# The products with w and u in the chunked delta-rule scan: one product of 128 columns with w, products with u in turn

## The chip, the cores and the metric

The kernel runs on one core of a Trainium2 chip. The metric is device time in microseconds (us), the median of three runs. Its engines in the profile are PE (TensorE matmul; PEld is its weight load), DVE (VectorE), ACT (ScalarE), POOL (GpSimd) and SP (SyncE, which here issues most DMAs). A float32 matmul appears in the trace as two records.

## The reference

A network of two blocks over 1024 tokens. The first block has gated scans, a dilated attention and a second layer of gated scans. The second block has, beside a pooling branch, a state-space scan (SSD) and a delta-rule scan (GDN) of six heads, both in two directions, then a router and experts. The change concerns the delta-rule scan, whose core is this:

```python
def gdn_chunked(q, k, v, g, beta, s0):
    ...
    u = jnp.einsum('bnhij,bnhjv->bnhiv', tm, vc * bc[..., None])
    w = jnp.einsum('bnhij,bnhjk->bnhik', tm, kb * jnp.exp(gc)[..., None])
    attn = jnp.einsum('bnhik,bnhjk->bnhij', qc, kc) * decay
    qg = qc * jnp.exp(gc)[..., None]
    kend = kc * jnp.exp(gc[..., -1:] - gc)[..., None]
    gend = jnp.exp(gc[..., -1])

    def step(s, inp):
        u_i, w_i, a_i, qg_i, ke_i, ge_i = inp
        v_new = u_i - jnp.einsum('bhlk,bhkv->bhlv', w_i, s)
        o_i = jnp.einsum('bhlk,bhkv->bhlv', qg_i, s) + jnp.einsum('bhij,bhjv->bhiv', a_i, v_new)
        s = s * ge_i[..., None, None] + jnp.einsum('bhlk,bhlv->bhkv', ke_i, v_new)
        return s, o_i
```

Chunks hold 64 tokens. The kernel folds w and u into matrices ahead of the walk over chunks: a chunk's end state is (exp(g_end) - ke^T w) S + ke^T u, and its outputs are (q exp(g) - A w) S + A u, with A the masked and decayed products of queries and keys.

## The kernel before, in words

All work is on one core. Matmul operands of the large projections are split into exact high and low parts (L139 to L141, three products for one). The framework schedules the instructions of the whole program into one fixed order per engine before the run, by its own estimate of times and with priority for what frees PSUM (`g.up()`); on the chip each engine runs its list in that order and waits on semaphores. Thus an edit in one function can shift instructions of others.

The stage in question begins near 2857 us of the span. `latent_mixers` calls `gdn_scan` for three pairs of heads (hp 0, 1, 2), `ssd` (the state-space scan), `gdn_finish` and then `MixersOut.group` for the output projection. `gdn_scan` loads keys and values and transposes them (L1556), multiplies queries with keys (L1571, tile hkq) and calls `prepare(d)` for both directions. `prepare` multiplies values and keys with the inverse T (L1603), so that huw holds u and hwb holds w as blocks of 128x128. From there:

- hke, keys decayed to the chunk's end (L1612, GpSimd), and hA, the diagonal of the state's factor (L1615);
- L1620: products of w with hke, 64 columns for each pair of chunks and head; L1623 subtracts them from hA;
- L1628: products of hke with u, halves of 64 partitions to the other half's partitions, copied into hB by L1635;
- the decay row of all chunks into hx (L1639 calls `gdn_rows`, four DMAs): exp and product with the queries (L1641, L1642, tile hQ), subtraction (L1643), mask (L1647, GpSimd), exp (L1649), product with hkq (L1650, GpSimd);
- L1654: products of w with those rows, subtracted from hQ by L1657; L1663: products of the rows with u, copied or added into hO by L1667 and L1669.

`carry` then walks over the chunks (L1692, L1694: one small product and one addition per chunk) and adds the states' part to the outputs (L1708). It runs beside the next pair's `prepare`. The state-space scan runs beside all of this (srow, sxw, sxb, sBC and L1245 to L1353). PSUM has three banks for the large projections (mm), one for the carry (a), and two each of o and tr, which `bank()` hands out in turn. Of `pool.tile` the argument bufs is the number of buffers of a tag: a writer waits until the reader of the buffer's earlier content is done.

Of the kernel before, what the change touches and what calls it, by code (L numbers as in the profile page):

```python
# [27 lines left out]
def dap(ap, dims, off=0):  # L28
    """A DRAM access pattern over ap's tensor, dims in elements."""
    return bass.AP(tensor=ap.tensor, offset=ap.offset + off, ap=[list(d) for d in dims])  # L30


class Ctx:
    """Engines, pools and constants shared by the parts."""
# [32 lines left out]
    def open_w(self):  # L67
        """Room for weight blocks, on the left; closed by ws.close()."""
        self.w = self.ws.enter_context(self.pool("w"))
# [18 lines left out]
    def psum(self, tag):  # L88
        """A bank of the tag's; work set aside to fill gaps has one of its own."""
        tag = self.aside or tag  # L90
        return self.ps.tile([P, 512], F32, name=tag, tag=tag, bufs=self.banks[tag])

    def psum_pool(self, name, **banks):
        """A pool of PSUM with the given numbers of banks, to be entered."""
# [7 lines left out]
    def load_w(self, blk, scale=None, k=4, n=256, units=2, colscale=None, pool=None, bufs=2):  # L102
        """A weight block [128, units*k, n] in DRAM, as exact float32r high and low parts."""
# [23 lines left out]
    def up(self):  # L127
        """For what frees PSUM."""
        return self.tc.high_priority()
# [5 lines left out]
    def mm3(self, ps, sta, mov, first=True, last=True):  # L135
        """ps += sum_k sta[k]^T mov[k], each a (hi, lo) pair of float32r operands."""
# [7 lines left out]
def fm(w, c, X, t0, n=512):  # L144
    """Operands of a feature-major product: 128 features at column c of block w, n tokens from t0."""
# [4 lines left out]
def tm(w, X, t0):  # L150
    """Operands of a token-major product: 128 tokens from t0, all columns of block w."""
# [3 lines left out]
class Gated:  # L155
    """The bidirectional gated scan of one head with its norm and gate, in units of n tokens.

    Backward units come first, from the last; then forward units, each followed by its outputs."""
# [11 lines left out]
    def unit(self, d, u, q, k, lg):  # L170
        """Direction d (0 forward, 1 backward), unit u; q, k, lg: [128 keys, n], lg: log gates / gs.
        Returns the forward outputs' decayed q."""
# [19 lines left out]
        # decays of the chunks, and the factors that carry q and k over neighbouring ones  # L192
# [18 lines left out]
        # states  # L211
# [30 lines left out]
        # products within the groups  # L242
# [21 lines left out]
    def out(self, u, qd, St, G, y):  # L264
        """Outputs of unit u into y [128 tokens, group, Vd]: head rms norm and gate."""
# [48 lines left out]
def put_y(g, pool, ydram, chunk, t0, src, tag="y_hl", bufs=1):  # L314
    """A piece of y^T, 128 features, tokens from t0: split exactly and kept in DRAM."""
# [6 lines left out]
def attention_pair(g, pool, ydram, pair, qs, qps, kT, gate, vd, bias, spread, before):  # L322
    """Two heads (128 features) of the dilated attention, from feature-major q (times -1/8), per head with the
    other's rows zero (qps: room for it by residues, likewise), k and silu(gate); vd: v in DRAM [1024, 512]; bias[h][p]: minus the biases, tiles [128, 256] or [128, 64].
    Returns what is left to do, the sum of the patterns; before: what the pair before left."""
# [8 lines left out]
    def permuted(d):  # L334
        """q and k with their tokens by residue of d"""
# [8 lines left out]
    # values, tokens on partitions in each pattern's order  # L344
# [122 lines left out]
    # weights of the patterns, in tokens' order: rows (h, j), j the block of 128 tokens  # L467
# [40 lines left out]
    def rest():  # L508
        # the weights, one row per 128 tokens, brought to the head's partitions by a product
# [16 lines left out]
def load_xT(g, pool, src):  # L526
    """x^T [1024, 1024] as eight chunks of features, exact high and low parts."""
# [29 lines left out]
def rel_bias(g, pool):  # L557
    """Minus the relative biases per head and pattern: tiles [query, key - query + 64]."""
# [13 lines left out]
    # a copy of each row per query, so that a pitch one shorter reads them shifted  # L572
# [21 lines left out]
def sigmoid(g, dst, src):  # L594
    """1 / (1 + exp(-src)), by the functions that share a table with the scans' own."""
# [16 lines left out]
class Layer0:  # L612
    """Layer 0: the gated scans' heads, and what the attention takes, into DRAM: per pair of heads q, k and gate by
    features; v by tokens; the biases."""

    def __init__(self, g, es, X, ydram):
# [6 lines left out]
        # low-rank gate inputs, split and stacked for one pass: rows hi, hi, lo  # L623
# [23 lines left out]
    def feature(self, dst, w, evict):  # L647
        """128 features into DRAM"""
# [6 lines left out]
    def inputs(self, c):  # L655
        """A pair's part of what the attention takes, and half of the values or of the gates."""
# [16 lines left out]
    def project(self, h):  # L673
        """A head's projections into DRAM"""
# [62 lines left out]
    def heads(self, hs, after, side="left"):  # L737
        """The scans of some heads; after(h) adds what may fill their gaps."""
# [36 lines left out]
class OutProj:  # L775
    """z = alpha x + y W, over groups of chunks of 128 features."""
# [6 lines left out]
    def load(self, chunks, pool=None, parts=1):  # L783
        """[y^T of the chunk, its weights], each high and low parts; pool: for further weights."""
# [39 lines left out]
    def last(self, chunks, more, pool, finish):  # L824
        """Chunks, some more with their weights in pool; finish(tok) when a tile of tokens is done."""
# [8 lines left out]
def layer_norm(g, zp, zt, gain, bias):  # L834
    """zt [128 tokens, 1024] in place."""
# [16 lines left out]
def to_feature_major(g, zt, tok, X, tags=("a", "o")):  # L852
    """Transpose 128 tokens [128, 1024] into the chunks X (exact high and low parts, or whole)."""
# [12 lines left out]
def hgrn(g, hp, X, ydram, aside):  # L866
    """Layer 1: twelve heads of 128 keys and values."""
# [992 lines left out]
class MixersOut:  # L1860
# [44 lines left out]
    def close(self):  # L1905
        self.es.close()
# [539 lines left out]
```

## Time and profile before

| | |
|---|---|
| runs | 3773.04, 3778.67, 3780.81 us; median 3778.67 us |
| profiled execution | span 3765.8 us; no time of its own beside the span is listed |
| PE busy | 3383.4 us, 90% of the span |
| DVE, ACT, POOL busy | 2579.5, 1618.4, 1444.7 us |
| DMA | 461.05 MB, mean 122 GB/s |
| scan stage | about 2860 to 3240 us |

A timeline row is a run of like instructions, with its start, the time from that start to the end of the last, the engine, the line, the tiles (out<-in), the shape and the number of records; in brackets the engine's idle time before it and what ended it. Matmuls are pipelined, so the start of the next row tells more of the pace than the duration. PEclk is the granted clock: 1.0 is 2.4 GHz and 0.5 is 1.2 GHz.

### The profile page before, as it was taken

The page shows a single profiled execution, that of the slowest core. Times are in us where ns is not written, and L with a number is a line of the kernel's source. Part 1 is how long each engine was busy: PE and PEld are TensorE (multiplying, and loading weights), DVE is VectorE, ACT ScalarE, POOL GpSimd, SP SyncE. Part 2 cuts the span into 40 slices and gives each one's busy share as a digit, 9 for nine tenths or more (in the row PEclk, how much of TensorE's full clock was granted, in tenths as well). Part 3 has the DMA queues.
Part 4 walks back from the last instruction along what each step waited for, and adds up shares of the span by engine and source line. Part 5 has one row for each costly group of instructions (what it writes and reads, how often), then busy time and mean ns, then how long its engine had stood idle before and what let it go on. Part 6 is the DMA issues. An engine that isn't in the chain of part 4 may idle for free.

```text
span 3765.8 us, 59868 instructions
## 1 busy us (share of the span) xinstructions
PE 3383.4 (90%) x21896; PEld 2754.0 (73%) x21896; DVE 2579.5 (68%) x5580; ACT 1618.4 (43%) x3340; POOL 1444.7 (38%) x1437
## 2 busy tenths in 40 slices
PE   7998998999988999999999999688896879858897
PEld 6886886777667888888898977566675868636665
DVE  4767664265476685977767686669995565578787
ACT  3443333444624454545545451344443331235565
POOL 4556664000023233434333331623213563245553
PEclk9998999999898999999999999889896889869999
DMA  5222244252333111111111234224337465578994
GB/s 182 75 82 90 88 136 139 79 174 66 89 119 106 64 65 59 50 59 48 50 43 63 68 123 148 81 87 133 105 106 174 111 157 182 214 214 291 299 326 152
DMA packets 374051, 461.05 MB, mean 122 GB/s; under 512 B 150483, under 2 KB 280787, under 8 KB 373756
## 3 DMA queue, kind: packets, MB, share of 16 engines
q1 hardware_dynamic: 359916, 407.93, 34.3%
q0 software_dynamic: 13840, 49.29, 4.4%
q8 instruction: 173, 2.83, 0.3%
q14 instruction: 122, 1.00, 0.1%
HBM read 357.57 MB, written 104.27 MB: 123 GB/s over the span
## 4 chain that ended last, share of the span: by engine, by line
PE 61%; DVE 16%; issue 7%; DMA 6%; POOL 4%; ACT 4%; SPq 2%; DVEq 0%; POOLq 0%; ACTq 0%
PE mm L139 12%; PE mm L140 12%; PE mm L141 12%; DVE cacc L1137 2%; PE a L247 2%; DVE elo L2015 2%; PE o L225 1%; DMA srow<-rdsl 1%; PE o L276 1%; PE a L214 1%; PE a L141 1%; PE a L251 1%; PE a L140 1%; PE o L280 1%; PE o L278 1%
## 5 line engine op out<-in xcount | busy, mean ns | idle before, releaser
L116 POOL TENSOR_TENSOR wlo<-wraw,whi 128x1024 fp32r<-128x1024 f32 (+1 forms) x131 | 329.0, 2516 | 537.1 <-ACT whi L115 532.4
L2013 ACT CAST ehi<-eraw 128x1024 fp32r<-128x1024 f32 x192 | 200.3, 1050 | 148.7 <-PE a L141 95.9
L139 PE MATMUL mm<-x1h,whi 128*128 128x512 f32 x576 | 237.4, 412 | 7.9 <-DVE G L913 3.5
L140 PE MATMUL mm<-x1l,whi 128*128 128x512 f32 x576 | 234.6, 407 | 2.5 <-DVE x1l L133 2.5
L141 PE MATMUL mm<-x1h,wlo 128*128 128x512 f32 x576 | 234.8, 408 | 0.0
L139 PE MATMUL mm<-whi,x1h 128*128 128x256 f32 x768 | 222.2, 289 | 0.0
L141 PE MATMUL mm<-whi,x1l 128*128 128x256 f32 x768 | 219.8, 287 | 0.0
L140 PE MATMUL mm<-wlo,x1h 128*128 128x256 f32 x768 | 219.6, 286 | 0.0
L2015 DVE TENSOR_TENSOR elo<-eraw,ehi 128x1024 fp32r<-128x1024 f32 x138 | 193.3, 1435 | 31.6 <-ACT ehi L2013 31.2
L115 ACT CAST whi<-wraw 128x1024 fp32r<-128x1024 f32 (+1 forms) x131 | 136.1, 1040 | 167.1 <-PE mm L140 96.9
L2017 POOL TENSOR_TENSOR elo<-eraw,ehi 128x1024 fp32r<-128x1024 f32 x54 | 138.2, 2565 | 167.4 <-ACT ehi L2013 153.2
L139 PE MATMUL mm<-whi,xh 128*128 128x256 f32 x640 | 185.2, 290 | 0.0
L140 PE MATMUL mm<-wlo,xh 128*128 128x256 f32 x640 | 183.9, 288 | 0.5 <-POOL wlo L116 0.5
L141 PE MATMUL mm<-whi,xl 128*128 128x256 f32 x640 | 183.2, 286 | 0.0
L139 PE MATMUL mm<-x2h,whi 128*128 128x512 f32 x400 | 165.4, 413 | 13.0 <-ACT cu L1129 8.8
L140 PE MATMUL mm<-x2l,whi 128*128 128x512 f32 x400 | 164.9, 412 | 0.0
L141 PE MATMUL mm<-x2h,wlo 128*128 128x512 f32 x400 | 163.2, 409 | 0.8 <-POOL wlo L116 0.8
L139 PE MATMUL mm<-whi,yin 128*128 128x512 f32 x352 | 149.4, 428 | 14.4 <-DVE z L816 6.9
L816 DVE TENSOR_TENSOR z<-z,mm 128x512 f32<-128x512 f32 x144 | 97.7, 682 | 86.8 <-PE mm L141 86.4
L139 PE MATMUL mm<-xh,whi 128*128 128x512 f32 x336 | 138.0, 411 | 19.3 <-ACT whi L115 16.2
L239 POOL TENSOR_TENSOR u_qh<-u_qa,facX 128x256 f32<-128x256 f32 x64 | 71.3, 1114 | 202.7 <-DVE u_qa L236 172.5
L139 PEld LDWEIGHTS mm<-whi,x1h 128*128 128x128 f32 x768 | 146.9, 191 | 1.1
(756 smaller groups left out, 10832.0 us busy)
## 6 DMA issues: line engine op xcount, KB each, us to landing
eraw<-in_we_gate_dram SPq DMA_DIRECT2D x64, 512.0 KB
eraw<-in_we_up_dram SPq DMA_DIRECT2D x64, 512.0 KB
eraw<-in_we_down_dram SPq DMA_DIRECT2D x64, 512.0 KB
yin<-yd POOLq DMA_DIRECT2D x29, 1024.0 KB, 9.1
aw<-in_ada_w_dram SPq DMA_DIRECT2D x96, 256.0 KB
yd<-y_hl SPq DMA_DIRECT2D x80, 256.0 KB
wraw<-in_w_dram SPq DMA_DIRECT2D x25, 512.0 KB
wraw<-in_w_out_dram SPq DMA_DIRECT2D x24, 512.0 KB
```

Source lines behind the costliest of these rows:

```text
L115: nc.scalar.copy(hi[:, :sz], raw[:, :sz])
L116: nc.gpsimd.tensor_tensor(lo[:, :sz], raw[:, :sz], hi[:, :sz].bitcast(F32), op=ALU.subtract)
L139: nc.tensor.matmul(ps, sh, mh, start=first and i == 0, stop=False)
L140: nc.tensor.matmul(ps, sh, ml, start=False, stop=False)
L141: nc.tensor.matmul(ps, sl, mh, start=False, stop=last and i == n - 1)
L239: nc.gpsimd.tensor_tensor(v3(qh, 32), v3(qa, 32), bcast(fqh, nck, 32), op=ALU.mult)
L247: nc.tensor.matmul(ap[:, o:o + P], w(kt, 0, P), w(qt, 0, P), start=True, stop=True)
L816: nc.vector.tensor_add(zz, zz, ps)
L1137: nc.vector.scalar_tensor_tensor(acc, u[:, i:i + n], cw[:, i:i + 1], acc, op0=ALU.mult, op1=ALU.add)
L2013: nc.scalar.copy(hi, raw)
L2015: nc.vector.tensor_sub(lo, raw, hi.bitcast(F32))
L2017: nc.gpsimd.tensor_tensor(lo, raw, hi.bitcast(F32), op=ALU.subtract)
```

## The change

In `prepare`, keys and rows lie side by side in one tile of the latents' scan (tag hke, 8 KB per partition instead of 4, still one buffer), and one product with w of 128 columns serves both. The row's chain (load, exp, subtraction, mask, exp, product) moves ahead of that product, and its last step writes into the shared tile. The products with u for the state (L1655 after) and for the outputs (L1658 after) alternate chunk by chunk and head by head in two banks. In the context's scan, which needs no outputs, the products stay as they were. Two buffer counts shrink: hf from 2 to 1, and the raw weights of the output projection (mraw) from 3 to 2. Everything else in the diff removes comments.

```diff
-        f = pool.tile([P, 3, ncp, 2], F32, name="hf", tag="hf", bufs=2)
+        f = pool.tile([P, 3, ncp, 2], F32, name="hf", tag="hf", bufs=1)
...
-        ke = t4("hke")
+        kinds = 1 if fin is not None else 2
+        kr = big("hke", [ncp, 2, kinds, 64])
+        ke = kr[:, :, :, 0]
         nc.gpsimd.tensor_tensor(ke, kt, bc(f[:, 0]), op=ALU.mult)
+        if fin is None:
+            row = gdn_rows(g, pool, n, rows, hp, d, 0, "hx", 2)
+            Q = big("hQ", [2, ncp, 64], 4)
+            nc.scalar.activation(Q, row, AF.Exp)
+            nc.vector.tensor_mul(Q, Q, qE)
+            nc.vector.tensor_sub(row, row, hc(col))
...
+            at = kr[:, :, :, 1]
+            nc.gpsimd.tensor_tensor(at.rearrange("p c h i -> p h c i"), row, kq, op=ALU.mult)
         A = t4("hA", two)
...
+        per = 4 // kinds
+        for q0 in range(0, ncp, per):
+            mm = min(per, ncp - q0)
+            ps = bank()
+            wd = kinds * 64
+            for i in range(mm * 2):
+                cp, h = q0 + i // 2, i % 2
+                nc.tensor.matmul(ps[:, i * wd:(i + 1) * wd], wb[:, cp * 2 + h], kr[:, cp, h], start=True, stop=True)
+            p5 = ps[:, :mm * 2 * wd].rearrange("p (c h x i) -> p c h x i", h=2, x=kinds, i=64)
+            with g.up():
+                nc.vector.tensor_sub(A[:, q0:q0 + mm], A[:, q0:q0 + mm], p5[:, :, :, 0])
+                if fin is None:
+                    Qs = Q[:, :, q0:q0 + mm].rearrange("p h c i -> p c h i")
+                    nc.vector.tensor_sub(Qs, Qs, p5[:, :, :, 1])
         for q0, mm in step4:
             ps = bank()
+            po = bank() if fin is None else None
             for i in range(mm * 2):
                 cp, h = q0 + i // 2, i % 2
-                nc.tensor.matmul(ps[:, i * 64:i * 64 + 64], wb[:, cp * 2 + h], ke[:, cp, h], start=True, stop=True)
...
+                io = slice(i * 64, i * 64 + 64)
                 for e in range(2):
+                    nc.tensor.matmul(ps[half[1 - e], io], ke[half[e], cp, h], u(e, cp, h), start=True, stop=True)
+                if fin is None:
+                    for e in range(2):
+                        nc.tensor.matmul(po[half[e], io], at[half[e], cp, h], u(e, cp, h), start=True, stop=True)
...
-        nc.gpsimd.tensor_tensor(row, row, kq, op=ALU.mult)
-        for h in range(2):
-            ps = bank()
-            for cp in range(ncp):
-                nc.tensor.matmul(ps[:, cp * 64:cp * 64 + 64], wb[:, cp * 2 + h], row[:, h, cp], start=True, stop=True)
...
-                raw = zp.tile([P, 512], F32, name="mraw", tag="mraw", bufs=max(nb, 2))
+                raw = zp.tile([P, 512], F32, name="mraw", tag="mraw", bufs=2)
```

PE's order in the first pair of heads, first direction, before (here one row is one instruction, x the number of them):

```order
L1620 MATMUL tr<-hke,hwb 128x64 x8
L1628 MATMUL o<-huw,hke 64x64 x16
L1248 MATMUL mm<-ident,sXB 128x128 x3
L1254 MATMUL mm<-ident,sXB 128x128 x2
L1620 MATMUL tr<-hke,hwb 128x64 x8
L1628 MATMUL o<-huw,hke 64x64 x2
L1692 MATMUL a<-hS,hA 64x64 x2
L1628 MATMUL o<-huw,hke 64x64 x14
L1265 MATMUL mm<-sxw,sxb 128x192 x2
L1654 MATMUL tr<-hx,hwb 128x64 x8
L1654 MATMUL o<-hx,hwb 128x64 x8
L1663 MATMUL tr<-huw,hx 64x64 x16
```

The same place in the changed kernel, where L1641 is the product with w, L1694 the carry, and L1655 and L1658 are the products with u:

```order
L1265 MATMUL mm<-sxw,sxb 128x192 x2
L1641 MATMUL tr<-hke,hwb 128x128 x4
L1641 MATMUL o<-hke,hwb 128x128 x4
L1641 MATMUL tr<-hke,hwb 128x128 x4
L1641 MATMUL o<-hke,hwb 128x128 x3
L1694 MATMUL a<-hS,hA 64x64 x2
L1641 MATMUL o<-hke,hwb 128x128
L1655 MATMUL tr<-huw,hke 64x64 x4
L1658 MATMUL o<-huw,hke 64x64 x4
L1655 MATMUL tr<-huw,hke 64x64 x2
L1658 MATMUL o<-huw,hke 64x64 x2
```

All products with w now stand together, and those with u follow in turns of two; the state-space products that stood among them come before.

GpSimd's order from the first pair's masks on, before (hke is the next direction's in the fourth row):

```order
L1647 AFFINE_SELECT hx<-hx 64x1024 x2
L1300 AFFINE_SELECT srow_29889<-srow_29889 128x768
L1300 AFFINE_SELECT srow_29964<-srow_29964 128x768
L1262 TENSOR_TENSOR sxw<-sxb,sw 128x384
L1650 TENSOR_TENSOR hx<-hx,hkq 128x1024
L1612 TENSOR_TENSOR hke<-hk,hf 128x1024
L1647 AFFINE_SELECT hx<-hx 64x1024 x2
L1595 TENSOR_TENSOR huw<-hv,rtgl 128x8x64 x2
L1650 TENSOR_TENSOR hx<-hx,hkq 128x1024
```

The same in the changed kernel, with L1626 the masks, L1630 the product with hkq and L1616 the keys:

```order
L1300 AFFINE_SELECT srow_29940<-srow_29940 128x768
L1626 AFFINE_SELECT hx<-hx 64x1024 x2
L1262 TENSOR_TENSOR sxw<-sxb,sw 128x384
L1630 TENSOR_TENSOR hke<-hx,hkq 128x2x8x64
L1626 AFFINE_SELECT hx<-hx 64x1024 x2
L1595 TENSOR_TENSOR huw<-hv,rtgl 128x8x64 x2
L1616 TENSOR_TENSOR hke<-hk,hf 128x16x64
L1630 TENSOR_TENSOR hke<-hx,hkq 128x2x8x64
L1262 TENSOR_TENSOR sxw<-sxb,sw 128x384
```

The second direction's keys moved behind its masks and its huw, next to the product that fills the other half of the same tile.

SP's order at the stage's start, before (lk and lv are the scan's keys and values, rdsl the decay rows of the state-space scan):

```order
L1510 DMA gT_28476<-gR 128x1024
L1225 DMA sS_29545<-sstates 128x384
L1245 DMA sXB<-lx 128x5x128
L1289 DMA sBC<-lx 128x7x128
L1296 DMA srow_29742<-rdsl 128x6x128
L1296 DMA srow_29749<-rdsl 128x6x128
L1552 DMA hx<-lk_25932 128x1024
L1552 DMA hx<-lv_25935 128x1024
```

And in the changed kernel:

```order
L1296 DMA srow_29718<-rdsl 128x6x128
L1296 DMA srow_29725<-rdsl 128x6x128
L1289 DMA sBC<-lx 128x7x128
L1296 DMA srow_29783<-rdsl 128x6x128
L1296 DMA srow_29790<-rdsl 128x6x128
L1510 DMA gT_28476<-gR 128x1024
L1245 DMA sXB<-lx 128x5x128
L1257 DMA sxbt_29530<-sxb 128x640
L1296 DMA srow_29865<-rdsl 128x6x128
L1552 DMA hx<-lk_25932 128x1024
L1552 DMA hx<-lv_25935 128x1024
```

Three more rows of the state-space scan and another of its inputs moved ahead of the scan's first keys.

## Rows read from the trace of the kernel before

**Rows 1.** From the page: busy time and share per engine

```profile
span 3765.8 us, 59868 instructions
PE 3383.4 (90%) x21896; PEld 2754.0 (73%) x21896; DVE 2579.5 (68%) x5580; ACT 1618.4 (43%) x3340; POOL 1444.7 (38%) x1437
```

**Rows 2.** Windows: us, busy (instructions) of PE, PEld, DVE, ACT, POOL; PEclk; DMA share; GB/s

```profile
2860.00:2900.00 40.00, 15.40 (x112) 13.18 (x113) 20.29 (x33) 9.80 (x22) 19.17 (x14) 0.56 0.94 191
2900.00:2960.00 60.00, 52.70 (x532) 49.37 (x526) 30.53 (x44) 19.77 (x40) 25.02 (x18) 0.72 0.47 112
3040.00:3080.00 40.00, 21.70 (x167) 18.35 (x163) 22.73 (x38) 11.13 (x21) 21.96 (x26) 0.73 0.65 181
3080.00:3150.00 70.00, 68.58 (x826) 62.59 (x825) 45.14 (x69) 27.55 (x56) 39.81 (x33) 0.88 0.68 209
```

**Rows 3.** Chain of waits, 2860 to 3260: start, us, what it is

```profile
2863.25 13.89 DMA hx<-lk
2888.50 4.80 DMA hx<-lk
3042.89 9.04 DMA srow<-rdsl
```

**Rows 4.** Timeline of PE, first pair: start, us, engine, line, operation, out<-in, records, [idle]

```profile
2902.12 1.90 PE L1620 MATMUL tr<-hke,hwb 128*128 128x64 f32 x16
...
2917.20 3.62 PE L1654 MATMUL o<-hx,hwb 128*128 128x64 f32 x16
2920.75 1.97 PE L1663 MATMUL tr<-huw,hx 64*64 64x64 f32 x32
...
2931.05 1.22 PE L1620 MATMUL tr<-hke,hwb 128*128 128x64 f32 x9 [1.79 <-DVE hwb L1609]
```

**Rows 5.** By tile (hke): matmul records, durations in ns, first and last start

```profile
L1620 PE MATMUL tr<-hke,hwb x192: 217/275/473, 2902.1 to 3136.3; 128*128 128x64 f32 x192
```

**Rows 6.** Timeline of PE, third pair, second direction, at full clock

```profile
3126.47 1.05 PE L1603 MATMUL tr<-huw,hTb 128*128 128x128 f32 x8
3127.36 1.06 PE L1603 MATMUL o<-huw,hTb 128*128 128x128 f32 x8
...
3131.66 1.89 PE L1620 MATMUL tr<-hke,hwb 128*128 128x64 f32 x16
3133.48 1.15 PE L1628 MATMUL o<-huw,hke 64*64 64x64 f32 x32
```

**Rows 7.** Timeline of PE: output products between carry steps; then carry steps alone

```profile
2986.28 0.27 PE L1663 MATMUL tr<-huw,hx 64*64 64x64 f32 x2
...
2986.52 0.23 PE L1692 MATMUL a<-hB,hA 64*64 64x64 f32 x2
2986.56 0.63 PE L1663 MATMUL tr<-huw,hx 64*64 64x64 f32 x16
...
3098.14 0.45 PE L1692 MATMUL a<-hB,hA 64*64 64x64 f32 x8
```

**Rows 8.** Timeline of POOL at the stage's start

```profile
2883.22 1.81 POOL L1305 TENSOR_TENSOR srow<-srow,srow 128x768 f32<-128x768 f32 x1
...
2911.33 2.35 POOL L1650 TENSOR_TENSOR hx<-hx,hkq 128x1024 f32<-128x1024 f32 x1
2913.63 2.22 POOL L1612 TENSOR_TENSOR hke<-hk,hf 128x1024 f32<-128x1024 f32 x1
```

**Rows 9.** Timeline of PE ahead of the router's first product

```profile
3225.65 0.39 PE L140 MATMUL mm<-mlo,yin 128*128 128x512 f32 x1
...
3226.10 0.39 PE L139 MATMUL mm<-mhi,yin 128*128 128x512 f32 x1
...
3239.54 0.61 PE L2159 MATMUL o<-rw,shb 128*128 128x16 f32 x2 [11.79 <-DVE shb L2158]
```

**Rows 10.** By tile (hA): Vector's subtractions from the product with w, in ns

```profile
L1623 DVE TENSOR_TENSOR hA<-hA,tr x12: 675/687/689, 2906.2 to 3136.6; 128x512 f32<-128x512 f32 x12
L1623 DVE TENSOR_TENSOR hA<-hA,f x6: 393/418/422, 2115.1 to 2263.6; 128x256 f32<-128x256 f32 x6
```

More of the change, by code (lines that the diff above doesn't have):

```diff
@@ L1610, in prepare @@
         u = lambda e, cp, h: uw[cp // nh][half[e], cp % nh, h, 0:64]
-        ke = t4("hke")
+        kinds = 1 if fin is not None else 2
+        kr = big("hke", [ncp, 2, kinds, 64])
+        ke = kr[:, :, :, 0]
         nc.gpsimd.tensor_tensor(ke, kt, bc(f[:, 0]), op=ALU.mult)
+        if fin is None:
[4 more added lines that the diff above has]
+            nc.vector.tensor_sub(row, row, hc(col))
+            r3 = row.rearrange("p h c i -> p (h c) i")
+            s = 1 if d == 0 else -1
+            for e in range(2):
+                nc.gpsimd.affine_select(r3[half[e]], r3[half[e]], pattern=[[0, m], [s, 64]], compare_op=ALU.is_ge,
+                                        fill=NEG, base=0, channel_multiplier=-s)
+            nc.scalar.activation(row, row, AF.Exp)
+            at = kr[:, :, :, 1]
+            nc.gpsimd.tensor_tensor(at.rearrange("p c h i -> p h c i"), row, kq, op=ALU.mult)
@@ L1616, in prepare @@
         for q0, mm in step4:
             ps = bank()
+            po = bank() if fin is None else None
             for i in range(mm * 2):
                 cp, h = q0 + i // 2, i % 2
-                nc.tensor.matmul(ps[:, i * 64:i * 64 + 64], wb[:, cp * 2 + h], ke[:, cp, h], start=True, stop=True)
-            As = flat(A[:, q0:q0 + mm])
-            with g.up():
-                nc.vector.tensor_sub(As, As, ps[:, :mm * P])
-            ps = bank()
-            for i in range(mm * 2):
-                cp, h = q0 + i // 2, i % 2
+                io = slice(i * 64, i * 64 + 64)
@@ L1627, in prepare @@
                 for e in range(2):
-                    nc.tensor.matmul(ps[half[1 - e], i * 64:i * 64 + 64], ke[half[e], cp, h], u(e, cp, h),
-                                     start=True, stop=True)
+                    nc.tensor.matmul(ps[half[1 - e], io], ke[half[e], cp, h], u(e, cp, h), start=True, stop=True)
+                if fin is None:
+                    for e in range(2):
+                        nc.tensor.matmul(po[half[e], io], at[half[e], cp, h], u(e, cp, h), start=True, stop=True)
@@ L1636, in prepare @@
                                    ps[half[1 - e], :mm * P].rearrange("p (c i) -> p c i", i=P))
-        if fin is not None:
-            return A, None
-        row = gdn_rows(g, pool, n, rows, hp, d, 0, "hx", 2)
-        Q = big("hQ", [2, ncp, 64], 4)
-        nc.scalar.activation(Q, row, AF.Exp)
-        nc.vector.tensor_mul(Q, Q, qE)
-        nc.vector.tensor_sub(row, row, hc(col))
-        r3 = row.rearrange("p h c i -> p (h c) i")
-        s = 1 if d == 0 else -1
-        for e in range(2):
-            nc.gpsimd.affine_select(r3[half[e]], r3[half[e]], pattern=[[0, m], [s, 64]], compare_op=ALU.is_ge,
-                                    fill=NEG, base=0, channel_multiplier=-s)
-        nc.scalar.activation(row, row, AF.Exp)
-        nc.gpsimd.tensor_tensor(row, row, kq, op=ALU.mult)
-        for h in range(2):
-            ps = bank()
-            for cp in range(ncp):
-                nc.tensor.matmul(ps[:, cp * 64:cp * 64 + 64], wb[:, cp * 2 + h], row[:, h, cp], start=True, stop=True)
-            Qh = Q[:, h].rearrange("p c i -> p (c i)")
-            with g.up():
-                nc.vector.tensor_sub(Qh, Qh, ps[:, :ncp * 64])
-        for q0, mm in step4:
-            ps = bank()
-            for i in range(mm * 2):
-                cp, h = q0 + i // 2, i % 2
-                for e in range(2):
-                    nc.tensor.matmul(ps[half[e], i * 64:i * 64 + 64], row[half[e], h, cp], u(e, cp, h), start=True, stop=True)
-            Os = flat(O[:, q0:q0 + mm])
-            with g.up():
-                if d == 0:
-                    nc.scalar.copy(Os, ps[:, :mm * P])
-                else:
-                    nc.vector.tensor_add(Os, Os, ps[:, :mm * P])
-        return A, Q
+                if fin is None:
+                    Os = flat(O[:, q0:q0 + mm])
+                    if d == 0:
+                        nc.scalar.copy(Os, po[:, :mm * P])
+                    else:
+                        nc.vector.tensor_add(Os, Os, po[:, :mm * P])
+        return (A, None) if fin is not None else (A, Q)
     B = big("hB", [m, 2, 64], 1 if fin is not None else 2)
```

## The prediction

> **What bounds the kernel now.** I read the page first: TensorE (PE) is busy 90% of the span [rows 1], so matmul time is worth money in general, but this change touches only the delta-rule scan of the second block, some 380 us near 3000 us. So the second view was the table of stretches there [rows 2]. The reader is to see that it is not one regime. From 2860 to 2900 us PE works 15.4 of 40 us and the DMA engines are 94% busy: transfers set the pace. From 2900 to 2960 PE is busy 52.7 of 60 us at a granted clock of 0.72. From 3040 to 3080 PE works only 21.7 of 40 us. From 3080 to 3150 it is full (68.6 of 70), and it is idle for most of 3220 to 3240. Third, the chain of waits inside the stage [rows 3]: it runs through a load of keys at 2863.25 and later through loads of the state-space scan's decay rows (srow); the 9.04 us one stands for five such pieces of 6.5 to 9.6 us between 3007 and 3076. A PE saving is therefore worth full price in the third pair of heads, most of its price in the first, and little in the second, which the state-space scan follows.
>
> **The change part by part.**
>
> Product with w. Before, 6 calls of prepare (3 pairs, 2 directions) each run 32 products of 64 columns, 192 in all; the trace shows two records each, 192 for the keys on L1620 [rows 5] and as many on L1654. After, 96 products of 128 columns. What counts is the price of one record. At full clock 16 records of 64 columns take from 3131.66 to 3133.48, 1.82 us or 0.114 each, while 8 records of 128 columns on the same kind of 128x128 weight take from 3126.47 to 3127.36, 0.89 us or 0.111 each [rows 6]. Twice the columns cost the same, so halving the records halves the time. At the lower clock 16 records take 3.55 us (2917.20 to 2920.75) [rows 4]. The 24 groups of 16 (L1620 and L1654) add up as 17 at about 1.9 us and 7 at about 3.5 us: 57 us before, 28.5 after. Saved: 11 us in the first pair, where the low clock falls, 7.8 in the second, 9.7 in the third.
>
> Here the Trainium skill, "TensorE: Matmul & The Clock Gate", section "Back-to-back issue gap", speaks against the change: its gap for an isolated matmul grows with the columns (N / 2.4 ns), by which a product of 128 columns costs twice one of 64 and the saving would be 0. The same section says that beside weight loads the gap is set by both; [rows 6] side with that.
>
> Products with u. The numbers stay (24 groups of 32 records, 768, on L1628 and L1663); only their order moves. Each is 64x64, a quarter of the array. Before, the state's products use two quarters in turn (rows of one half to columns of the other), the outputs' products the other two, in separate runs: 32 records in 1.15 us, 0.036 each (3133.48) [rows 6]. After, the two kinds alternate, so all four quarters are used in turn. The trace has this pattern by accident: where carry steps fall between output products, 8 records of each go from 2986.28 to 2986.56, 16 records in 0.28 us or 0.0175 each [rows 7], and another such place, among the query-key products, reads the same. At 0.0175 the 768 records lose half of their 32 us (17 groups of 32 at 1.1, 7 at 1.9): 16 us gained. The other bound is the slowest 64x64 stream at full clock, the carry steps' own 8 records in 0.45 us [rows 7], 0.056 each: 15 us lost. I take 12 gained, nearer the mixed rows, since they are the same operands' shapes and quarters.
>
> The same page of the Trainium skill says under "The mechanism" (its list of what overlaps) that a weight load overlaps a running matmul only when the row group differs. Row halves alternate before and after alike, so by it nothing would be gained here and the sum would be 12 us smaller; [rows 7] show the halving.
>
> Evictions. Vector does 8 subtractions of 256 elements per prepare instead of 4 of 512. 512 take 0.687 us, 256 (in the context scan) 0.418 [rows 10]: 8 x 0.418 - 4 x 0.687 = 0.6 us per prepare, 3.6 in all, beside 52.7 us of PE where Vector is at 30.5 of 60 [rows 2]; strided operands may add as much again. Costed at nothing; the price if that cover fails is 3.6.
>
> The row chain now comes first. A is taken from the same product as the outputs' part, so it waits for the decay row's load, two selects, exp and the multiplication on GpSimd. In the first pair that multiplication ends at 2913.68 [rows 8], while the keys' product began at 2902.12 [rows 4]: about 6.7 us of PE work (L1620 and L1628, 2902.12 to 2909.2) move behind 2913.7. After that, W at low clock is 7.1 us instead of 14.2 and the products with u 4 instead of 7.6, so the first direction ends near 2924, where it ended before. Queued on PE behind that wait are carry-independent SSD products, and the next direction.
>
> One buffer for keys and rows. The second direction's keys and rows may be written only when the first's products with u are done: 2.22 + 2.35 us on GpSimd [rows 8]. Before, the keys of direction two were already written at 2915.8. Cover: the second direction's u and w products and their copies, which end when L1620 starts, 2931.05 [rows 4], against 2924 + 4.6 = 2928.6. Nothing, then, with 2.4 us to spare; uncovered it is 4.6 x 5 = 23 us.
>
> First pair in sum: -11 for w, -5 for u, +6.7 for the work that waits: about -10. Start of the stage. On SP the scan's first key load stood behind two state-space rows and was issued at 2863.25 [rows 3]; now it stands behind five, and the fifth needs a buffer that the first rows' multiplication on GpSimd frees. That ran at 2883.22 before [rows 8], behind copies that waited for these very keys (landed at 2877.14); I put it near 2876 now. So the key load goes out some 13 us later, but the bytes ahead of the last key load (4.80 us at 2888.50 [rows 3]) are the same ones in another order, at 94% busy engines. Bounds: 5 gained, 10 lost; I take +3.
>
> Second pair: -7.8 and -3.5, of which the idle stretch behind it takes all but 5. Third pair: -9.7 and -3.5 with PE full, less 1 for the same buffer wait: -12.
>
> The end of the stage. Behind the last transposition for head pair three, PE waits for the router's row: 11.79 us idle before 3239.54 [rows 9]. The changed order puts 51 of the output projection's products there instead of 21; 30 more at 0.225 us (3225.65 to 3226.10 for two) are 6.8 us of work that fill the gap. Part of that is how the third pair's saving arrives, so I add only -3.
>
> Small edits: a third buffer of projection weights (mraw) and a second of factors (hf) are given up. The factors' wait lies on Vector, ahead of a stage that waits for the inverse anyway. The weights can cost 0 to 5 us; I take +2.
>
> Sum: -10 + 3 - 5 - 12 - 3 + 2 = -25. All instructions from the stage's start to the end are scheduled anew, and the order before this stage changes in places too; I take 3 us off for what that loses, -22. The profiled execution has a span of 3765.8 us [rows 1]; the three timed runs have their median at 3778.67, 12.9 above, for what lies around it. Predicted: 3778.7 - 22 = 3757, with its own range 3741 to 3769.
>
> **The rivals.**
>
> Absorbed. The state-space scan's srow loads and the start's transfers set the stage's length, and PE work only shrinks the idle. For it: 18.3 us of idle in 3040 to 3080 and the loads on the chain. Against: from 3080 on PE is full for 140 us. Only half of the third pair's saving and none of the rest: about -6, 3773.
>
> Slower. GpSimd becomes the gate: keys and row wait for the last product with u, and GpSimd has state-space selects and multiplications queued between. It decides once the wait passes the 2.4 us of cover; at the full 4.6 us for five of six prepares, plus 6.7 for the first, it costs 30 against a gain of 20 (w in pairs one and three): +10, 3789. Against it: GpSimd is busy only 25 of 60 us there.
>
> Columns count. If the price went by columns, the product with w would save nothing and the alternation little: about -3, 3776. This is the first rule of the Trainium skill ("TensorE: Matmul & The Clock Gate", "Back-to-back issue gap") that was weighed above. [Rows 6] speak against it.
>
> Everything arrives: 28.5 + 16 with the order no worse: -42, 3737.
>
> That the change doesn't do what it says is excluded for the product (96 fewer); for the alternation the order shows it in turn, two by two.
>
> **How the numbers follow.** Forecast 0.50, absorbed 0.20, slower 0.12, columns 0.08, everything 0.10. A measurement tells about 0.2%, 7.6 us, from no change. Faster: 0.47 of the forecast, 0.06 of absorbed, all 0.10: 0.63. Slower: 0.12, with 0.04 of absorbed and columns: 0.16. The rest, 0.21, is the same. The range reaches from the everything case to half-way between absorbed and slower, with the start's bound: 3737 to 3785.
>
> **What would show it.** Right: the w product with 192 records at 0.11 us at full clock; 64 records with u in about 1.2 us; PE full from the third pair's start, and the idle before the router's first product under 6 us. Wrong: the gap between the first direction's last product with u and the second's first with w above 7 us; or records of 128 columns at 0.2 us at full clock; or PE idle near 3040 to 3080 grown by what was saved before it.

## The result: 0.55% faster, and the profile after

The changed kernel takes 3755.3 us (median of 8 runs, 3748.08 to 3762.35) against 3773.93 for the kernel before in 8 runs (3762.17 to 3783.30). The ratio is 0.9945, with a 95% interval of 0.9928 to 0.9961: 18.6 us faster. Forecast was 3757, and 22 us faster.

The page of the profile after; the first row answers to [rows 1], PE having 33 us less to do:

```profile
span 3746.0 us, 59511 instructions
PE 3350.0 (89%) x21704; PEld 2716.6 (73%) x21704; DVE 2586.0 (69%) x5604; ACT 1618.4 (43%) x3340; POOL 1452.7 (39%) x1437
```

The table of stretches after, which answers to [rows 2] (us, busy time and instructions of PE, PEld, DVE, ACT, POOL, then PEclk, DMA share, GB/s):

```profile
2860.00:2900.00 40.00, 15.46 (x60) 12.35 (x59) 18.88 (x24) 10.14 (x20) 22.74 (x17) 0.54 0.82 189
2900.00:2960.00 60.00, 43.98 (x642) 39.09 (x641) 42.98 (x69) 28.02 (x60) 29.80 (x22) 0.88 0.63 151
3040.00:3080.00 40.00, 34.17 (x323) 29.65 (x322) 29.59 (x49) 15.88 (x33) 30.64 (x26) 0.87 0.64 143
3080.00:3150.00 70.00, 51.32 (x637) 41.08 (x635) 38.27 (x70) 18.90 (x39) 28.96 (x25) 0.83 0.53 184
```

The reader is to see three things. In 2900 to 2960 PE is busy 8.7 us less, at a clock of 0.88 instead of 0.72. The idle stretch of 3040 to 3080 is filled (34.17 instead of 21.70), since the later work arrives earlier. And 3080 to 3150, which was full, is now idle for 18.7 of 70 us: a new wait.

Milestones, each read as the last end or first start of a line on PE in the two timelines (one execution each):

| end of, or start of | before | after | difference |
|---|---|---|---|
| inverses' last product (L1506) | 2858.5 | 2860.1 | +1.6 |
| first full product with w | 2902.1 | 2914.0 | +11.9 |
| first pair's last product with u | 2952.4 | 2936.6 | -15.8 |
| second pair's last product with u | 3044.1 | 3029.1 | -15.0 |
| third pair's last product with u | 3143.4 | 3109.8 | -33.6 |
| third pair's first carry step | 3151.5 | 3126.6 | -24.9 |
| third pair's last transposition | 3222.8 | 3206.1 | -16.7 |
| router's first product | 3239.5 | 3222.8 | -16.7 |
| span | 3765.8 | 3746.0 | -19.8 |

PE's timeline of the first pair, first direction, after (answers to [rows 4]):

```profile
2911.52 1.65 PE L1265 MATMUL mm<-sxw,sxb 128*128 128x192 f32 x4 [5.36 <-POOL sxw L1262]
2914.00 2.08 PE L1641 MATMUL tr<-hke,hwb 128*128 128x128 f32 x8 [0.84 <-POOL hke L1630]
2915.87 1.80 PE L1641 MATMUL o<-hke,hwb 128*128 128x128 f32 x8
2917.51 1.06 PE L1641 MATMUL tr<-hke,hwb 128*128 128x128 f32 x8
...
2919.95 0.27 PE L1655 MATMUL tr<-huw,hke 64*64 64x64 f32 x2
2919.98 0.27 PE L1658 MATMUL o<-huw,hke 64*64 64x64 f32 x2
...
2922.93 1.16 PE L1603 MATMUL tr<-huw,hTb 128*128 128x128 f32 x8 [0.82 <-POOL huw L1595]
...
2928.62 1.16 PE L1641 MATMUL tr<-hke,hwb 128*128 128x128 f32 x8 [1.31 <-POOL hke L1630]
```

The product with w is 2914.00 to 2919.95, and 128 records with u lie between 2919.95 and about 2921.9, 0.015 us each. The first eight records of the product with w still take 1.87 us (lower clock), the next eight 1.64, the third eight 0.89. In the last row PE waited 1.31 us for GpSimd, which had itself waited for the first direction's products with u:

```profile
2921.32 3.01 POOL L1595 TENSOR_TENSOR huw<-hv,rtgl 128x512 f32<-128x512 f32 x2 [2.22 <-PE o L1658]
2924.29 1.90 POOL L1616 TENSOR_TENSOR hke<-hk,hf 128x1024 f32<-128x1024 f32 x1
2926.16 2.41 POOL L1630 TENSOR_TENSOR hke<-hx,hkq 128x1024 f32<-128x1024 f32 x1
```

By tile, the product with w after, in ns, 192 records for the 384 of before [rows 5]:

```profile
L1641 PE MATMUL tr<-hke,hwb x96: 273/275/579, 2914.0 to 3100.6; 128*128 128x128 f32 x96
L1641 PE MATMUL o<-hke,hwb x96: 275/275/553, 2915.9 to 3103.8; 128*128 128x128 f32 x96
```

Vector's subtractions from it, in ns (answers to [rows 10]); the rows' half (L1647) costs the same, 0.41:

```profile
L1644 DVE TENSOR_TENSOR hA<-hA,tr x12: 405/412/422, 2916.6 to 3100.9; 128x256 f32<-128x256 f32 x12
L1644 DVE TENSOR_TENSOR hA<-hA,o x12: 407/418/422, 2917.7 to 3104.1; 128x256 f32<-128x256 f32 x12
```

The new wait is the load of the finished second pair's gate (lg, a DMA of 512 KB), which stands in the chain of waits of 3040 to 3262 (start, us, what):

```profile
3106.18 17.66 DMA fg<-lg
```

It was issued behind six loads of x for the output projection (z, 512 KB each, from 3101.22). PE's timeline there:

```profile
3109.28 0.48 PE L1658 MATMUL o<-huw,hke 64*64 64x64 f32 x4 [3.24 <-issue]
...
3124.68 1.12 PE L1736 MATMUL a<-ident,hO 128*128 128x128 f32 x4 [6.10 <-DVE fg L1739]
3126.57 0.70 PE L1694 MATMUL a<-hS,hA 64*64 64x64 f32 x8 [0.78 <-DVE fg L1739]
```

The transposition at 3124.68 waited for Vector's product with that gate (fg), and the carry of the third pair, which shares PSUM's bank a with it, follows at 3126.57. Before, the gate was late as well (issued 3135.95), but PE was full with other work until 3143. The end of the stage answers to [rows 9]:

```profile
3205.52 0.60 PE L1736 MATMUL a<-ident,hO 128*128 128x128 f32 x4
...
3222.80 0.61 PE L2161 MATMUL o<-rw,shb 128*128 128x16 f32 x2 [5.07 <-DVE shb L2160]
```

PE's idle time ahead of the router's first product fell from 11.79 to 5.07 us, but from the last transposition to it is 16.7 us in both kernels: SP issues the router's rows after the store of the finished rows, and the projection's products only filled the gap.

### The profile page after: what moved, and what is told of

Same layout as the page of the kernel before. It is cut to its first block, busy times and chain, and to the rows that moved or that the text cites. A ratio compares the mean times of both kernels' runs of the same rounds, so it can differ in the third digit from the quotient of the medians.

```text
span 3746.0 us, 59511 instructions
## 1 busy us (share of the span) xinstructions
PE 3350.0 (89%) x21704; PEld 2716.6 (73%) x21704; DVE 2586.0 (69%) x5604; ACT 1618.4 (43%) x3340; POOL 1452.7 (39%) x1437
## 4 chain that ended last, share of the span: by engine, by line
PE 58%; DVE 19%; issue 7%; DMA 7%; POOL 4%; ACT 3%; SPq 1%; DVEq 0%; POOLq 0%; ACTq 0%
PE mm L139 12%; PE mm L140 12%; PE mm L141 12%; DVE elo L2017 2%; PE a L247 2%; DVE cacc L1137 2%; PE o L225 1%; DMA srow<-rdsl 1%; PE a L141 1%; PE a L140 1%; PE o L276 1%; PE a L139 1%; PE a L251 1%; PE a L214 1%; PE a L399 1%
## 5 line engine op out<-in xcount | busy, mean ns | idle before, releaser
L2017 DVE TENSOR_TENSOR elo<-eraw,ehi 128x1024 fp32r<-128x1024 f32 x138 | 198.3, 1472 | 32.9 <-ACT ehi L2015 32.5
L139 PE MATMUL mm<-whi,yin 128*128 128x512 f32 x352 | 151.3, 433 | 12.2 <-DVE z L816 6.6
```

The lines of the kernel that those rows point to most:

```text
L139: nc.tensor.matmul(ps, sh, mh, start=first and i == 0, stop=False)
L2017: nc.vector.tensor_sub(lo, raw, hi.bitcast(F32))
```

## The experiments

All ratios are to the kernel before, from five rounds, with the 95% interval; where two runs stand in different series, their ratios compare better than their times. The framework schedules each kernel anew, so an edit also moves other instructions; that is part of what was learned. "Stage" is the time from the last L1506 record to the router's first product in the profile, one execution each: 381.1 us before, 362.7 after. e7, whose time is that of the kernel before, reads 382.4.

| run | us | ratio (interval) | stage |
|---|---|---|---|
| e1_u_apart | 3745.16 | 0.9928 (0.9903 to 0.9954) | 356.7 |
| e2_w_apart | 3783.43 | 1.0019 (1.0004 to 1.0034) | 397.0 |
| e3_both_apart | 3795.04 | 1.0054 (1.0034 to 1.0073) | 402.3 |
| e4_buffers | 3761.08 | 0.9971 (0.9953 to 0.9990) | 373.5 |
| e5_gate_hq | 3733.39 | 0.9886 (0.9863 to 0.9908) | 346.1 |
| e6_gate_u_apart | 3763.95 | 0.9959 (0.9944 to 0.9973) | 369.4 |
| e7_mraw2 | 3776.13 | 0.9995 (0.9980 to 1.0009) | 382.4 |
| e8_gate_before | 3782.60 | 1.0012 (0.9996 to 1.0027) | 384.9 |
| e9_hf1 | 3758.98 | 0.9957 (0.9941 to 0.9973) | 363.3 |
| e10_gate_w_apart | 3783.02 | 1.0023 (1.0005 to 1.0042) | 389.5 |

PE's time in the two products, summed over the stage from the start of each row to the start of the next, without PE's idle time; and how many of the records with w began at the lower clock:

| kernel | with w, us | with u, us | with w at the lower clock |
|---|---|---|---|
| before | 57.5 | 32.5 | 115 of 384 |
| e4 (before, both counts) | 54.7 | 33.0 | 88 of 384 |
| e7 (before, raw weights) | 57.9 | 32.5 | 119 of 384 |
| e8 (before, gate early) | 53.5 | 32.6 | 78 of 384 |
| e9 (before, hf 1) | 49.4 | 28.4 | 38 of 384 |
| after | 30.7 | 19.1 | 60 of 192 |
| e1 (u apart) | 27.7 | 21.8 | 48 of 192 |
| e5 (gate early) | 30.7 | 18.5 | 68 of 192 |
| e6 (gate early, u apart) | 27.4 | 21.3 | 44 of 192 |
| e2 (w apart) | 69.1 | 21.5 | 233 of 384 |
| e3 (both apart) | 66.2 | 27.0 | 196 of 384 |
| e10 (gate early, w apart) | 68.3 | 18.9 | 227 of 384 |

**The products with u, one after the other (e1).** From the changed kernel:

```diff
-                if fin is None:
-                    for e in range(2):
-                        nc.tensor.matmul(po[half[e], io], at[half[e], cp, h], u(e, cp, h), start=True, stop=True)
+            if fin is None:
+                for i in range(mm * 2):
+                    cp, h = q0 + i // 2, i % 2
+                    io = slice(i * 64, i * 64 + 64)
+                    for e in range(2):
+                        nc.tensor.matmul(po[half[e], io], at[half[e], cp, h], u(e, cp, h), start=True, stop=True)
```

> The changed kernel with one edit: per four chunk pairs the products with u for the state come in one run and those for the outputs in the next, instead of in turn. Theory (alternation halves their pace): 128 records with u per prepare take about 4.6 us at full clock (0.036 each) instead of 1.95 (0.015 each) as in the first direction of the changed kernel; the stage loses some 12 to 16 us of PE time and the kernel comes 5 to 12 us above 3755, near 3763. Rival (the gain is the new order and the merged product alone): pace and time stay, 3755 within 4 us.

Both missed: it came out at 3745.16, if anything faster than the changed kernel (the intervals overlap). PE's timeline of its first pair:

```profile
2923.19 0.97 PE L1655 MATMUL tr<-huw,hke 64*64 64x64 f32 x26
2923.95 0.27 PE L1661 MATMUL o<-huw,hke 64*64 64x64 f32 x2
2924.00 0.28 PE L1655 MATMUL tr<-huw,hke 64*64 64x64 f32 x3
...
2924.12 0.80 PE L1661 MATMUL o<-huw,hke 64*64 64x64 f32 x21
...
2924.88 0.80 PE L1655 MATMUL tr<-huw,hke 64*64 64x64 f32 x21
...
2925.64 0.98 PE L1661 MATMUL o<-huw,hke 64*64 64x64 f32 x27
2926.87 1.16 PE L1603 MATMUL tr<-huw,hTb 128*128 128x128 f32 x8 [0.25 <-POOL huw L1595]
```

The 128 records need 3.4 us (2923.19 to about 2926.6) where the alternation needs 1.95. Inside a run 26 records take 0.76 us, 0.029 each; the starts of single records are two every 0.058 us here, in the kernel before and in e9 alike, and four every 0.058 us in turns. e1 is not the clean opposite, though: the scheduled order mixes the ends of its runs (from 2923.95), and there four start in that time as well. Over the stage the difference is only 2.7 us (21.8 against 19.1), not 12. In the first pair the turns save 1.3 and 1.1 us, one for each direction; in the second they save nothing (8.4 us in the changed kernel, 8.2 in e1), as 101 of the changed kernel's 256 records ran at the lower clock there and none of e1's did. In this kernel's scheduled order the gate was issued at 3109.75, ahead of the loads of x (first at 3110.74), and the third pair's carry took 35.0 us (3132.5 to 3167.4) instead of the changed kernel's 47.0 (3126.6 to 3173.6). So the alternation is real in PE's records, but the kernel is no slower without it: it is not shown to have made the changed kernel faster.

**The product with w in two instructions (e2), and both edits (e3).** In e2:

```diff
-                nc.tensor.matmul(ps[:, i * wd:(i + 1) * wd], wb[:, cp * 2 + h], kr[:, cp, h], start=True, stop=True)
+                for x in range(kinds):
+                    nc.tensor.matmul(ps[:, i * wd + x * 64:i * wd + x * 64 + 64], wb[:, cp * 2 + h], kr[:, cp, h, x],
+                                     start=True, stop=True)
```

> The changed kernel with one edit: the product with w is two instructions of 64 columns again (keys, then rows, side by side in the same bank, same evictions), 192 instead of 96. Theory (records cost the same at 64 and 128 columns): 384 records instead of 192 at 0.11 us, 22 us more PE time in the three pairs, and the kernel 8 to 18 us above 3755, near 3767. Rival (columns set the price): the product takes as long as before, and the time stays at 3755 within 4 us.

> The changed kernel with both edits of e1 and e2: the order of the changed kernel (row chain first, one tile, one buffer), but as many records as before and no alternation. Theory (the gain is PE time in the stage, the new order costs a little): no gain left, 3774 to 3784. Rival (the order of the state-space scan and of the loads brings the gain): 3755 to 3762.

Measured 28 us above the changed kernel for e2 and 40 for e3, both slower than before. The new order with its buffer counts is a loss by itself (e3, 0.54% slower, with 196 of 384 records of the product with w at the lower clock where the kernel before has 115), and the merged product is what pays for it. The loss in e2 is larger than the theory's 8 to 18, because PE's time with w went from 30.7 to 69.1 us: twice the records and, beyond that, more of them at the lower clock (table above). e10, below, shows it on rows.

**The buffer counts alone (e4), and each by itself (e7, e9).** From the kernel before; e4 has both lines, e7 the second, e9 the first:

```diff
-        f = pool.tile([P, 3, ncp, 2], F32, name="hf", tag="hf", bufs=2)
+        f = pool.tile([P, 3, ncp, 2], F32, name="hf", tag="hf", bufs=1)
...
-                raw = zp.tile([P, 512], F32, name="mraw", tag="mraw", bufs=max(nb, 2))
+                raw = zp.tile([P, 512], F32, name="mraw", tag="mraw", bufs=2)
```

> The kernel before with the two buffer counts of the change alone (factors 2 to 1, raw weights 3 to 2). Theory: 0 to 4 us slower than before, 3774 to 3778. Rival (the buffer counts shift the order of the whole program enough to make the difference): 10 us or more to either side.

> The kernel before with the raw weights' buffers from 3 to 2 alone. Theory (two buffers of raw weights hold back products of the output projection, which let the third pair's scan go first, and this gave e4 its 12 us): near e4, 3758 to 3767. Rival (it is the factors' single buffer): 3772 to 3778.

> The kernel before with the factors' buffers (hf) from 2 to 1 alone. Theory (after e7: the single buffer of the factors shifts the scheduled order of the stage, and that is e4's gain): near e4, 3758 to 3768. Rival (only both counts together give it): 3772 to 3778.

The side edits were no side matter: the factors' single buffer alone makes the kernel before 0.43% faster (e9), the raw weights' alone does nothing (e7; its theory fell). For e9 the granted clock shows where most of it lies (last but two of the columns). First the kernel before, first pair, in stretches of 5 us:

```profile
2905.00:2910.00 5.00, 4.10 (x61) 3.63 (x57) 3.19 (x6) 3.50 (x6) 2.58 (x3) 1.00 0.78 155
2910.00:2915.00 5.00, 2.46 (x10) 1.96 (x11) 1.64 (x3) 2.24 (x4) 5.00 (x4) 0.69 0.95 196
2915.00:2920.00 5.00, 5.00 (x26) 5.00 (x25) 2.96 (x3) 0.82 (x1) 2.50 (x3) 0.50 0.25 60
2920.00:2925.00 5.00, 5.00 (x71) 4.76 (x71) 1.90 (x3) 2.06 (x3) 2.60 (x3) 0.50 0.26 55
```

And e9 at the same place of its own span, some 10 us later:

```profile
2910.00:2915.00 5.00, 5.00 (x67) 4.87 (x64) 4.08 (x4) 2.54 (x7) 1.82 (x2) 1.00 0.75 204
2915.00:2920.00 5.00, 5.00 (x79) 4.54 (x74) 1.95 (x4) 2.54 (x5) 3.76 (x3) 1.00 0.84 123
2920.00:2925.00 5.00, 4.32 (x49) 4.11 (x49) 4.14 (x2) 2.64 (x5) 4.40 (x3) 1.00 0.27 66
```

Before, PE works 2.46 of the 5 us from 2910, and the clock is at its lower level for the products that follow, from 2912 to 2953 except 2925.6 to 2932.4. The profiles of e7 and e8, which also have two buffers of factors, show the same two stretches; with one buffer, e4 shows only the second and e9 neither. In e9 the order leaves 0.69 us of wait at that place, and the clock stays at 1.00. The two products together cost 13.5 us less in e9's first pair and 12.2 less over the stage (table above), most of the 16 us gained. In e4, with the same single buffer, they cost only 2.3 us less, and it is still some 11 us faster than the kernel before. So the clock accounts for e9's profile, one execution, and is not shown to be the whole of what the single buffer gives. Whether two buffers of factors would slow the changed kernel was not run.

**The gate early (e5), the same in e1 (e6) and in the kernel before (e8).** One edit in `gdn_finish`:

```diff
-    gt = pool.tile([P, T], F32, name="fg", tag="hx", bufs=2)
+    gt = pool.tile([P, T], F32, name="fg", tag="hq", bufs=1)
```

> The changed kernel with one edit: the gate of a finished pair is loaded into the queries' buffer (hq, free earlier) instead of one that the rows use, so that the second pair's gate load is queued ahead of the eight loads of x for the output projection. In the changed kernel that load took 17.66 us behind them, and the first carry step of the third pair started at 3126.6, 17 us after the last product with u. Theory (the late gate eats part of the gain): the carry starts within 8 us of that product and the kernel comes 6 to 12 us below 3755, 3743 to 3749. Rival (the projection's products or the carry bound the end anyway): 3755 within 4 us.

> The kernel before with e5's edit alone, the gate's load ahead of the loads of x. Theory (there the gate is hidden behind the third pair's products, which keep TensorE full until 3143): 3775 within 4 us. Rival (the early gate is worth as much in any order): 6 to 12 us faster, 3763 to 3769.

> The edits of e1 (products with u in two runs) and of e5 (gate into the queries' buffer) together. Theory (e1 was faster than the changed kernel because the late gate did not hold it): with the gate early, alternation should pay, so this is slower than e5 by 3 to 9 us, and no faster than e1: 3744 to 3752. Rival (two runs are better in themselves): faster than e5 and e1, 3735 to 3741.

e5 is the fastest version: 3733.39, its interval clear of the changed kernel's, some 22 us below it, where 6 to 12 were expected. SP's timeline shows the gate's load now ahead of all loads of x:

```profile
3074.96 0.33 SPq L1732 DMA_DIRECT2D fg<-lg  x1
...
3097.32 5.26 SPq L1896 DMA_DIRECT2D z<-x2d  x8
```

And the third pair's first carry step, with what it waited for:

```profile
3114.41 0.46 PE L1694 MATMUL a<-hS,hA 64*64 64x64 f32 x8 [0.78 <-DVE fg L1739]
```

It comes 9 us after the last product with u (3105.3), where it was 17 after; I had said within 8. That is some 8 of the 22 us; most of the rest lies in the third carry, 32 us instead of 47, and why that is shorter stays open. In the kernel before the same edit gains nothing (e8), as the theory had it: a late load costs only where PE has run out of other work. e6 went the theory's way and more than three times as far: two runs with the early gate take 3763.95, 31 us more than e5 and, by the ratios, some 12 more than e1, though those two intervals overlap. So the early gate gained in one order and not in two others. PE's time with u is only 2.8 us more than in e5 (21.3 against 18.5). Its third carry lasts 59 us (3132.0 to 3190.9) where e5's lasts 32 (3114.4 to 3146.5), and PE waits 12.0 us for the router's row again. Most of the 31 us is thus not the price of these instructions but goes with the scheduled order; which place decides between e1 and e6 stays open.

**The product with w apart, on the fastest version (e10).** e2's edit in e5:

> The fastest version so far (e5) with the product with w as two instructions of 64 columns again, as in e2. Theory (the merged product saves records and, as e2 and e3 show in the first pair, the full clock as well): 28 to 45 us slower than e5, 3761 to 3778, with the first pair's product at 0.21 to 0.22 us a record where e5 has about 0.11. Rival (e2's loss came from its order or the late gate): at most 22 us slower than e5, below 3756.

50 us slower than e5, so the rival falls, and the loss is larger than the theory's 45. PE's timeline of its first direction:

```profile
2915.58 3.25 PE L1642 MATMUL tr<-hke,hwb 128*128 128x64 f32 x14 [0.80 <-POOL hke L1630]
2918.62 3.19 PE L1642 MATMUL o<-hke,hwb 128*128 128x64 f32 x14
2921.61 1.92 PE L1642 MATMUL tr<-hke,hwb 128*128 128x64 f32 x8
```

14 records of 64 columns take 3.04 and 2.99 us, 0.216 each. The stretches around them in e10 (the products with w proper begin at 2915.58):

```profile
2908.00:2913.00 5.00, 1.23 (x8) 0.74 (x7) 4.27 (x5) 2.98 (x6) 3.66 (x4) 0.88 0.80 162
2913.00:2918.00 5.00, 4.07 (x16) 3.56 (x16) 3.15 (x4) 1.14 (x2) 2.45 (x2) 0.50 0.62 184
2918.00:2923.00 5.00, 5.00 (x25) 5.00 (x25) 1.74 (x5) 1.06 (x1) 2.28 (x2) 0.50 0.64 140
```

And the same place in e5, where the products have 128 columns:

```profile
2905.00:2910.00 5.00, 1.79 (x5) 1.29 (x5) 2.51 (x4) 2.11 (x2) 4.58 (x4) 0.72 0.77 202
2910.00:2915.00 5.00, 5.00 (x28) 5.00 (x29) 4.10 (x8) 0.01 (x1) 2.28 (x2) 0.60 0.72 179
2915.00:2920.00 5.00, 4.18 (x145) 3.73 (x145) 3.21 (x6) 3.65 (x6) 2.48 (x2) 1.00 0.22 34
```

Both kernels come out of a wait in which PE worked 1.2 or 1.8 of 5 us. With 128 columns a record the clock is at 1.00 in the third row; with 64 it is still at 0.50 there, and the products with w stay at it until 2928.5. So merging saves twice here: half the records, and the full clock for them and for the products with u behind them. It is not so in every pair: in the second of e10 the 64-column records ran at the full clock (7.8 and 7.2 us for 64 records).

## Why the prediction was right, and where its steps failed

**Right in time, in part by luck.** The forecast of 22 us met 18.6, but its terms missed to both sides. At the third pair's last product with u they come to 24 us (-10 + 3 - 5 - 12), and 33.6 were measured; of these, 16.9 were lost again before the router, which no term had.

- The product with w: 57 to 28.5 us forecast, 57.5 to 30.7 in the traces. [rows 6] were the right rows: eight records of 128 columns took 0.89 us from 2917.51, as there. That the merged product is needed is shown by e2 against the changed kernel, e3 against e1 and e10 against e5, where undoing it costs 28 to 50 us. By pairs the sum hid misses: 11, 7.8 and 9.7 us forecast, 14.5, 2.2 and 10.2 measured. The lower clock had moved. In the first pair it held 84 of 128 records before and 16 of 64 after, in the second none before and 44 of 64 after.
- The Trainium skill's rule that the columns set an isolated product's price ("TensorE: Matmul & The Clock Gate", "Back-to-back issue gap") does not describe these streams: 64 and 128 columns took 0.114 and 0.111 us a record. For products beside weight loads the same section says that both set the spacing, and with that the traces agree.
- The products with u: 16 us was the most, 12 taken; PE's time fell by 13.4 (32.5 to 19.1). But by e1 the turns give only 2.7 of it, and in time nothing that shows. e9 suggests some 4 by the clock. The rest is in the starts of single records: the pace inside a run is the same in e9 and e1, but in e9 many runs of 32 stand between products on 128x128 weights and lose about 0.15 us in changing over (the run at 2914.40 takes 1.07 us, where 16 pairs at 0.058 would take 0.93), while in e1 four runs stand together and their ends mix. The step that failed is the unit: 0.036 us a record was the price of a run with its ends, not of the pace that turns would halve.
- By the Trainium skill's rule on overlap by row groups (same page, "The mechanism"), as the prediction read it, the turns would have given nothing. The pace of 0.015 us against 0.029 disagrees with that reading.
- The first pair: forecast -10 and +3 for the start, measured -15.8 at its end. The start cost next to nothing: the key load went out 8 us later (2871.36), not 13, and GpSimd's product of the row chain ended at 2913.95 instead of 2913.68. The wait for that chain came as said (product with w at 2914.00, forecast after 2913.7). The step that failed is "W at low clock is 7.1 us": it took 5.95, and the second direction's 4.6 instead of 7.1, because the clock rose within the first 16 records, and the products with u then ran at the full clock. The mechanism was right and the clock was mis-sized.
- The one buffer did hold the second direction, a little: its product with w began at 2928.62, where the prediction had 2928.6 with cover until 2931.05, but the cover ended at 2927.3, so PE waited 1.31 us. That the times meet is luck: the products with u ended 2 us earlier than forecast, and GpSimd's product into huw (3.01 us), which the sum left out, came between. The rival by which GpSimd becomes the gate is out: from the first pair to the third PE waited for its product into the shared tile four times, 0.26 to 1.31 us, 2.7 in sum.
- Second pair -5, third -12: measured +0.8 and -18.6, right in sum alone. The second pair's records were at the lower clock, as said above. The idle stretch still did not swallow what came before it, because the state-space scan moved forward with it: its first product with its rows started at 2974.3 instead of 2993.4. The "absorbed" rival is thereby out. PE was not full from 3080, though, which had been named as a sign.
- What the prediction did not have: the gate's load. 8.7 of the 33.6 us were gone before the carry; in e5, with the gate early, the carry started some 8 us sooner after the last product with u. Another 8.2 went between the carry's start and the last transposition; why is not shown.
- "The end of the stage, -3" failed: the 30 products more filled the gap without shortening it, 16.7 us in both.
- "Small edits, +2": wrong in sign. The raw weights cost nothing (e7), and the factors' single buffer alone gains 16 us in the kernel before (e9). Against e9, the merged product and the turns bring the kernel only from 0.9957 to 0.9945, which these intervals do not separate. So it is not shown that the change beats its own side edit; it is shown that in its order the merged product is needed, and that with the gate early it is far ahead of e9. The single buffer and the early gate without the merged product were not run together.
- The 12.9 us between the profiled span and the median are not "what lies around it": each timed run is 2.1 us longer than its own span, and the rest is scatter between executions. The forecast difference does not use it.

## What to carry to other kernels

Two products with the same weights and few columns are one product, if a row of the trace shows that the record's price doesn't rise with the columns; look at the granted clock of the stretch as well, before and after the edit, since in e10 227 of 384 records ran at its lower level. When a stage's work gets shorter, look for loads that were late but covered, try them ahead of bulk loads, and measure: here it gained 22 us in one order and nothing in two others. Where a list scheduler orders the program, test the "harmless" buffer edits alone: here one moved as much time as the whole change.

## What the runs showed of the hardware that was not expected

In the first pair of e10, e2 and e3, after a wait, 55 to 62 of the 64 records with w of each direction were at the lower clock (0.216 us a record, 2915.58 to 2928.5 in e10); in the third pair's first direction the clock rose after 23 records in e3 and 45 in e10. The 128-column records on the same weights began at the lower clock too, for 16 to 24 of 32 in the first direction of the changed kernel, e1, e5 and e6, and were then at the full one (0.111 a record). Where PE had not waited before, as in [rows 6], streams of 64 columns ran at the full clock too. Four quarters of the array in turns reach 0.015 us a 64x64 record, half of the 0.029 inside a run on two quarters; the 0.036 of [rows 6] has the run's ends in it.
